# Preparing two neighbouring chunks of a DeltaNet scan as one pair, in tiles of eight heads

## The chip, the cores and the metric

One core of one Trainium2 chip runs the whole step. Its engines are called by short names throughout: PE is the matmul engine (TensorE), PEld its weight loads, DVE is VectorE, ACT is ScalarE, POOL is GpSimd, SP issues the DMAs. The metric is the device time of one execution in microseconds. Before the change the median of three runs is 2609.4 us (2607.69 to 2610.45).

## The reference

One layer of a hybrid backbone on 128 context tokens and 2048 latent tokens: a modulated RMSNorm, one input projection, then in parallel a bidirectional gated DeltaNet (4 heads of 128) and a gated MLP with spatial mixing, one output projection, then a squared-ReLU MLP of 1024 to 4096 and back. The change touches the DeltaNet alone:

```python
decay = jnp.where(incl, jnp.exp(jnp.where(incl, diff, 0.0)), 0.0)
a_mat = jnp.where(strict, jnp.einsum('bnhcd,bnhsd->bnhcs', k_beta, k) * decay, 0.0)
...
sol = lax.linalg.triangular_solve(a_mat + jnp.eye(DN_CHUNK, dtype=f32), rhs,
                                  left_side=True, lower=True, unit_diagonal=True)
...
qk = jnp.einsum('bnhcd,bnhsd->bnhcs', q, k) * decay
...
def step(S, xs):
    qd, kd, u_c, w_c, qk_c, gl = xs
    v_new = u_c - jnp.einsum('bhck,bhkv->bhcv', w_c, S)
    o = jnp.einsum('bhck,bhkv->bhcv', qd, S) + jnp.einsum('bhcs,bhsv->bhcv', qk_c, v_new)
    S = S * jnp.exp(gl)[..., None, None] + jnp.einsum('bhck,bhcv->bhkv', kd, v_new)
    return S, o
```

Per chunk and direction a triangular system is solved for each head (this needs nothing of the chunks before it), and then a short recurrence carries the state S from chunk to chunk. The kernel works with chunks of 128 tokens.

## The kernel before

The program has three stages: the input projection, the scan, the MLP. The trace has the scan's matmuls (those into the tile `pd`) from 462 to 1246 us. Only this stage is touched.

**Units.** There are 17 chunks and two directions d, so 34 units `unit(t, d)`. Each has a preparation (`prep`), which makes an explicit triangular inverse T for its four heads, and a recurrence (`scan`) of four steps. In the preparation, E holds the decays, KK the chunk's key products (with nbeta and the decay this becomes the negative triangular matrix, kept as the fp16 parts AH and AL), X and Y are the growing inverse and its transpose, P a scratch matrix, R a residual of one Newton step. The PE's groups in a preparation, with letters that this document uses for them, are

- **Y0**: four transposes of X into Y;
- five levels s = 2, 4, 8, 16, 32, each of a group **a** (four matmuls of AH with half of Y, 64 columns, L1065), a predicated copy by DVE into P (L1069), then groups **b** (P with X, L1076) and **c** (X with P, L1079), whose results ACT copies into Y (L1080) and X (L1081);
- the last level, 64, on quarters of the array: **m** (L1095) and **n** (L1103, L1105), matmuls of 64x64;
- **R** (eight matmuls, L1113 and L1114, DVE adds the identity, L1116) and **T** (five matmuls, L1122 and L1123, four ACT activations, L1126).

In this order each group waits for what DVE or ACT made of the group ahead of it. The four recurrence steps are called KS (state times keys, L992), TV (T times values), NS (new state) and O (output, L1179 and L1180); their operands are fp32.

**Fills.** Between these groups stand matmuls that nobody waits for at once: the gMLP's projections while the forward units run (L224 to L226 with `hH`, `hL`), the output projection while the backward units run (the same lines with `oH`, `oL`). A projection of one token tile is 24 matmuls of 512 columns, cut by `PARTS` into 9, 9 and 6; the output projection goes in pieces of 6.

**Order.** All steps are entered with a time in units (`at`, `spread`), sorted by it and recorded; `WINDOWS` holds the times. A unit's 18 preparation steps are spread from 2.46 to 0.03 units ahead of its recurrence, so that two or three units' preparations are interleaved. A scheduler then orders each engine's instructions by a timeline of its own; `emit` adds that a fill may not pass the last group of the preparation or recurrence that was entered ahead of it. DVE, ACT and POOL run their instructions strictly in the order that results.

**Buffers.** AH, AL, X and Y have three each (`BA`, `BX`), QK three, E, Es and KK share four. The five P tiles are shared by all units. They hold an identity, in which a level overwrites the same blocks each time; a unit that is the first of its direction (`fresh`) copies it anew.

Of the kernel before, what the change touches and what calls it, by code (L numbers as in the profile page):

```python
# [8 lines left out]
F32 = mybir.dt.float32  # L9
# [22 lines left out]
def interleave(*lists):  # L32
# [5 lines left out]
    for _, _, _, s in sorted(order, key=lambda e: e[:3]):  # L38
# [4 lines left out]
BA = 3  # L43
BX = 3
BT = 1
NS = 4
NE = 4
# [3 lines left out]
LATE = 0.5  # L51
PARTS = ((0, 3), (3, 6), (6, 8))
PL = 0
# [8 lines left out]
WINDOWS = [2.46, 0.03, -0.51, 1.06, -2.1, 18.16, 17.58, 18.3,  # L62
           2.63, -0.06, -0.18, 1.0, 1.36, 1.64, 1.66, 2.66, 3.17, 3.71]
# [3 lines left out]
def hybrid_step(  # L67
# [863 lines left out]
    with ExitStack() as ph:  # L931
# [17 lines left out]
        def f16(tag, bufs=1):  # L949
            return pp.tile([P, 4, P], F16, tag=tag, name=tag, bufs=bufs)  # L950
# [3 lines left out]

        def s32(name):
            return pp.tile([P, 4, P], F32, tag="e", name=name, bufs=NE)

# [6 lines left out]
        identq = f16("identq")  # L964
        V.tensor_copy(identq, bc4(ident16))
        pms = {s: f16(f"P{s}") for s in (2, 4, 8, 16, 32)}
# [15 lines left out]
        def unit(t, d, fresh=False, last=False):  # L982
# [11 lines left out]
            def prep_loads():  # L994
                u["gb"] = load_rows(g_d, t, d, "gr", 1, pp)
                u["KK"] = s32("KK")
                load(out=u["KK"], in_=kk_d[t])
                u["QK"] = q32("QK", 3)
                load(out=u["QK"], in_=qk_d[t])

            def scan_loads():
                for nm, src in (("kT", kT_d), ("qT", qT_d)):
                    u[nm] = q32(nm, 2)
                    load(out=u[nm], in_=src[:, :, t * P : (t + 1) * P])
                for nm, src in (("kt", kt_d), ("vt", vt_d)):
                    u[nm] = q32(nm, 2)
                    load(out=u[nm], in_=src[t * P : (t + 1) * P, :].rearrange("p (h d) -> p h d", h=H))
                u["eg"] = load_rows(eg_d, t, d, "eg", 3)
# [4 lines left out]
            @prep.append  # L1013
            def _():
                e = s32("E")
# [3 lines left out]
                es = s32("Es")  # L1019
                G.affine_select(out=es, in_=e, pattern=[[0, 4], [-sg, P]], compare_op=ALU.is_gt, fill=0.0,  # L1020
                                base=0, channel_multiplier=sg)
                G.affine_select(out=e, in_=e, pattern=[[0, 4], [sg, P]], compare_op=ALU.is_ge, fill=0.0,
                                base=0, channel_multiplier=-sg)
                u["Es"], u["E"] = es, e

            @prep.append
            def _():
                a = u["KK"]
                for h in range(H):
                    V.scalar_tensor_tensor(out=a[:, h, :], in0=a[:, h, :], scalar=col(nbeta, h),  # L1030
                                           in1=u["Es"][:, h, :], op0=ALU.mult, op1=ALU.mult)
# [3 lines left out]
            @prep.append  # L1035
            def _():
                u["AH"], u["AL"], u["X"] = f16("AH", BA), f16("AL", BA), f16("X", BX)
                A.copy(u["AH"], u["KK"])
                V.tensor_tensor(out=u["X"], in0=u["AH"], in1=bc4(sg2), op=ALU.mult)

            @prep.append
            def _():
                p = pd()
                for h in range(H):
                    T.matmul(p[:, h, :], u["X"][:, h, :], ident16, start=True, stop=True)
                u["Y"] = f16("Y", BX)
                A.copy(u["Y"], p)
                V.tensor_tensor(out=u["AL"], in0=u["KK"], in1=u["AH"], op=ALU.subtract)

            def level(s):  # L1050

                def half(ap, i):
                    return ap.rearrange("p h (a t b) -> p h a t b", t=2, b=s)[:, :, :, i, :]

                def packed(p, i):
                    return p[:, :, i * 64 : i * 64 + 64].rearrange("p h (a b) -> p h a b", b=s)

                yi = 1 - d

                @prep.append  # L1060
                def _():
                    p = pd()
                    pp, y = packed(p, 0), half(u["Y"], yi)
                    for h in range(H):
                        T.matmul(pp[:, h], u["AH"][:, h, :], y[:, h], start=True, stop=True)  # L1065
                    u["P"] = pms[s]
                    if fresh:
                        V.tensor_copy(pms[s], identq)
                    V.copy_predicated(out=half(u["P"], yi), mask=half(bc4(om[s]).bitcast(U16), yi), data=pp)  # L1069

                @prep.append
                def _():
                    p = pd()
                    py, px = packed(p, 0), packed(p, 1)
                    y, x, pm = half(u["Y"], yi), half(u["X"], 1 - yi), half(u["P"], yi)
                    pe = first_pe(lambda: [T.matmul(py[:, h], u["X"][:, h, :], pm[:, h], start=True, stop=True)  # L1076
                                           for h in range(H)])
                    for h in range(H):
                        T.matmul(px[:, h], u["P"][:, h, :], x[:, h], start=True, stop=True)  # L1079
                    A.copy(y, py)  # L1080
                    A.copy(x, px)  # L1081
                    if s == 8:
                        behind(lambda: V.tensor_tensor(out=u["QK"], in0=u["QK"], in1=u["E"], op=ALU.mult), pe)

            for s in (2, 4, 8, 16, 32):
                level(s)

            lo, hi = slice(0, 64), slice(64, P)
            ra, rb = (lo, hi) if d == 0 else (hi, lo)

            @prep.append
            def _():
                p = pd()
                for h in range(H):
                    T.matmul(p[ra, h, 0:64], u["AH"][rb, h, ra], u["Y"][rb, h, rb], start=True, stop=True)  # L1095
                u["P"] = f16("Pm", 1)
                A.copy(u["P"][ra, :, 0:64], p[ra, :, 0:64])

            @prep.append
            def _():  # L1100
                py, px = pd(), pd()
                for h in range(H):
                    T.matmul(py[ra, h, 0:64], u["X"][ra, h, ra], u["P"][ra, h, 0:64], start=True, stop=True)  # L1103
                for h in range(H):
                    T.matmul(px[rb, h, 0:64], u["P"][ra, h, 0:64], u["X"][ra, h, ra], start=True, stop=True)  # L1105
                A.copy(u["Y"][ra, :, rb], py[ra, :, 0:64])
                V.tensor_copy(u["X"][rb, :, ra], px[rb, :, 0:64])

            @prep.append
            def _():  # L1110
                p = pd()
                for h in range(H):
                    T.matmul(p[:, h, :], u["AH"][:, h, :], u["Y"][:, h, :], start=True, stop=False)  # L1113
                    T.matmul(p[:, h, :], u["AL"][:, h, :], u["Y"][:, h, :], start=False, stop=True)  # L1114
                u["R"] = f16("R", 1)
                V.tensor_tensor(out=u["R"], in0=p, in1=bc4(ident16), op=ALU.add)  # L1116

            @prep.append
            def _():
                p = pd()  # L1120
                for h in range(H):
                    T.matmul(p[:, h, :], u["X"][:, h, :], u["R"][:, h, :], start=h == 0, stop=False)  # L1122
                T.matmul(p, ident16, u["Y"], start=False, stop=True)  # L1123
                u["T"] = q32("T", BT)
                for h in range(H):
                    A.activation(u["T"][:, h, :], p[:, h, :], AF.Copy, scale=col(hbeta, h))  # L1126
# [15 lines left out]
            def _():  # L1142
                p = pd()
                pe = first_pe(lambda: quad(p, u["T"], u["vt"]))
                u["vn"] = q32("vn", BT)
# [51 lines left out]

        units = [unit(0, 0, True), unit(0, 1, True)] + [unit(t, 0, t == 1, t == NT - 1) for t in range(1, NT)]
        units += [unit(t, 1, t == NT - 1, t == 1) for t in range(NT - 1, 0, -1)]


# [216 lines left out]
        for i, u in enumerate(units):  # L1418
            w = p2 if i <= NT else p3
            at(i - 3 if i > PL else -12.5, u["prep_loads"])  # L1420
            at(i - 1, u["scan_loads"])
            n = len(u["prep"])
            for j, st in enumerate(u["prep"]):
                at(i - w[0] + (j + 0.5) * (w[0] - w[1]) / n, st, "prep")
# [36 lines left out]
        for j in range(len(wlist)):  # L1461
            at(-2 + 0.12 * j if j < KT else 16.4 + 0.12 * (j - KT), lambda j=j: split_next(j))
# [9 lines left out]
        spread(NT + 0.8, NT + 1.1, first, "fill")  # L1472
        spread(NT + 1.1, NT + 1.8, second, "fill")
        tend = max(e[0] for e in events if e[3] == "prep")
# [549 lines left out]
```

## Time and profile before

| what | value |
|---|---|
| median of the runs | 2609.4 us |
| the profiled execution | 2610.3 us, its span 2608.3 us |
| PE, PEld, DVE, ACT, POOL busy | 98%, 82%, 68%, 48%, 10% of the span |
| scan | 462 to 1246 us |

A row of a group gives the source line, engine, operation, output and inputs with shapes, the count, busy time, the mean of one in ns, and the idle time of the engine just before, with what ended it. In a timeline, the first column is the start in us and the second how long a row's instructions took together. A matmul's shown duration includes its way through the array, so a stream of them overlaps: their price is the distance from start to start. "PE busy" therefore also holds some waiting, and a group's idle time is a little less than what the wait cost.

### The profile page before, as it was taken

The page shows a single profiled execution, that of the slowest core. Times are in us where ns is not written, and L with a number is a line of the kernel's source. Part 1 is how long each engine was busy: PE and PEld are TensorE (multiplying, and loading weights), DVE is VectorE, ACT ScalarE, POOL GpSimd, SP SyncE. Part 2 cuts the span into 40 slices and gives each one's busy share as a digit, 9 for nine tenths or more (in the row PEclk, how much of TensorE's full clock was granted, in tenths as well). Part 3 has the DMA queues.
Part 4 walks back from the last instruction along what each step waited for, and adds up shares of the span by engine and source line. Part 5 has one row for each costly group of instructions (what it writes and reads, how often), then busy time and mean ns, then how long its engine had stood idle before and what let it go on. Part 6 is the DMA issues. An engine that isn't in the chain of part 4 may idle for free.

```text
span 2608.3 us, 44097 instructions
## 1 busy us (share of the span) xinstructions
PE 2563.6 (98%) x15330; PEld 2148.5 (82%) x15330; DVE 1771.7 (68%) x3587; ACT 1245.5 (48%) x3086; POOL 257.9 (10%) x478
## 2 busy tenths in 40 slices
PE   8999999999999999999999999999999999999998
PEld 4899999787888778778888888888887888888887
DVE  5767746666567878876588787677675545774875
ACT  4755555555555667764255553333342433242441
POOL 3112112111111122211000000000000000000000
PEclk9999999999999999999999999999999999999999
DMA  8966638655555667995778788545379978786773
GB/s 296 290 215 213 201 115 237 227 152 165 154 153 173 215 195 254 278 281 176 289 222 240 237 260 313 155 125 162 106 208 387 339 258 294 251 255 211 228 250 113
DMA packets 533860, 579.78 MB, mean 222 GB/s; under 512 B 35500, under 2 KB 366684, under 8 KB 530054
## 3 DMA queue, kind: packets, MB, share of 16 engines
q1 hardware_dynamic: 533638, 576.98, 69.2%
q8 instruction: 120, 1.97, 0.3%
q14 instruction: 102, 0.84, 0.1%
HBM read 397.62 MB, written 179.22 MB: 221 GB/s over the span
## 4 chain that ended last, share of the span: by engine, by line
PE 54%; DMA 5%; DVE 3%; ACT 2%; issue 1%; SPq 0%; DVEq 0%; POOLq 0%; POOL 0%; ACTq 0%
PE f L224 15%; PE f L225 15%; PE f L226 15%; PE pj L224 2%; PE pj L226 2%; PE pj L225 2%; DMA r<-in_w_ff_dram 1%; PE pd L992 1%; DMA x_d<-x 1%; DMA x<-x_d 1%; DMA traw<-in_w_ff_dram 1%; DMA zraw<-z_d 1%; PE pd L1179 0%; PE pd L1180 0%; DMA hop_d<-opL 0%
## 5 line engine op out<-in xcount | busy, mean ns | idle before, releaser
L224 PE MATMUL f<-hop,zH 128*128 128x512 f32 x960 | 373.6, 390 | 1.5 <-ACT zH L1527 1.4
L226 PE MATMUL f<-hop,zL 128*128 128x512 f32 x960 | 373.6, 390 | 0.0
L225 PE MATMUL f<-hop,zH 128*128 128x512 f32 x960 | 373.3, 389 | 0.1
L224 PE MATMUL f<-hop,wH 128*128 128x512 f32 x896 | 351.7, 393 | 1.0 <-ACT wH L1674 1.0
L225 PE MATMUL f<-hop,wH 128*128 128x512 f32 x896 | 349.0, 390 | 0.0
L226 PE MATMUL f<-hop,wL 128*128 128x512 f32 x896 | 344.0, 390 | 0.0
L1527 ACT CAST zH<-zraw 128x512 fp32r<-128x512 f32 x240 | 146.8, 620 | 284.6 <-DVE zraw L1521 83.9
L224 PEld LDWEIGHTS f<-hop,zH 128*128 128x128 f32 x960 | 180.2, 188 | 40.0 <-ACT zH L1527 2.8
L226 PEld LDWEIGHTS f<-hop,zL 128*128 128x128 f32 x960 | 180.2, 188 | 38.9 <-DVE zL L1521 1.7
L1521 DVE TENSOR_TENSOR zL<-zraw,zH 128x512 fp32r<-128x512 f32 x240 | 162.7, 688 | 71.6 <-ACT zH L1527 58.0
L225 PEld LDWEIGHTS f<-hop,zH 128*128 128x128 f32 x960 | 180.2, 188 | 37.6 <-DVE hop L1521 0.5
L224 PEld LDWEIGHTS f<-hop,wH 128*128 128x128 f32 x896 | 168.5, 188 | 35.8 <-ACT wH L1674 1.8
L226 PEld LDWEIGHTS f<-hop,wL 128*128 128x128 f32 x896 | 168.2, 188 | 35.6
L225 PEld LDWEIGHTS f<-hop,wH 128*128 128x128 f32 x896 | 168.6, 188 | 32.1
L226 PE MATMUL pj<-kH,wL 128*128 128x386 f32 (+2 forms) x568 | 190.6, 336 | 0.0
L224 PE MATMUL pj<-kH,wH 128*128 128x386 f32 (+2 forms) x568 | 189.2, 336 | 0.8 <-DVE cv L541 0.5
L225 PE MATMUL pj<-kL,wH 128*128 128x386 f32 (+2 forms) x568 | 189.4, 333 | 0.0
L182 POOL TENSOR_TENSOR r<-rsq,nhalf 128x1 f32<-128x1 f32 (+1 forms) x38 | 24.0, 631 | 1383.6 <-DVE rsq L181 1383.6
L1674 ACT CAST wH<-s 128x512 fp32r<-128x512 f32 x96 | 58.9, 620 | 171.4 <-DVE s L1521 158.1
L1069 DVE CAST_PREDICATED P<-om,pd 128x256 f16<-128x256 uint16 x170 | 72.2, 429 | 89.2 <-PE pd L1065 89.0
L541 DVE SCALAR_TENSOR_TENSOR cv<-pj,vec,cv 128x384 f32<-128x384 f32 (+2 forms) x164 | 87.2, 540 | 58.0 <-ACT cv L538 56.8
L224 PEld LDWEIGHTS pj<-kH,wH 128*128 128x128 f32 x568 | 107.1, 189 | 5.4 <-issue 5.0
(410 smaller groups left out, 5882.9 us busy)
## 6 DMA issues: line engine op xcount, KB each, us to landing
zraw<-z_d SPq DMA_DIRECT2D x212, 256.0 KB, 4.6
raw<-in_w_ff_dram SPq DMA_DIRECT2D x128, 256.0 KB, 4.6
hop<-hop_d SPq DMA_DIRECT2D x28, 1024.0 KB, 11.7
z_d<-c SPq DMA_DIRECT2D x96, 256.0 KB, 2.4
zraw<-s_d SPq DMA_DIRECT2D x96, 256.0 KB, 4.9
raw<-in_w_mod_dram SPq DMA_DIRECT2D x80, 256.0 KB, 4.6
r<-in_w_ff_dram SPq DMA_DIRECT2D x80, 256.0 KB, 5.5
s_d<-s SPq DMA_DIRECT2D x64, 256.0 KB, 3.0
```

The costliest lines, as they stand in the source:

```text
L182: G.tensor_tensor(out=out, in0=t[:np_, :n], in1=nhalf[:np_, :n], op=ALU.pow)
L224: T.matmul(ps, lh, rh, start=first and i == 0, stop=False, skip_group_check=more)
L225: T.matmul(ps, lh, rl, start=False, stop=False, skip_group_check=more)
L226: T.matmul(ps, ll, rh, start=False, stop=last and i == n - 1, skip_group_check=more)
L541: V.scalar_tensor_tensor(out=cv[:, o : o + m], in0=ps[:, s + sh : s + sh + m], scalar=convw[:, w, j : j + 1], in1=cv[:, o : o + m], op0=AL ...
L992: T.matmul(p[:, h, :], lhs[:, h, :], rhs[:, h, :], start=True, stop=True)
L1069: V.copy_predicated(out=half(u["P"], yi), mask=half(bc4(om[s]).bitcast(U16), yi), data=pp)
L1521: V.tensor_tensor(out=out, in0=a, in1=b, op=op)
L1527: A.copy(h, src)
L1674: A.copy(h, s2)
```

## The change

- `pair(us)` takes two neighbouring units and prepares them as one: AH, AL, X, Y, P and R are tiles of eight heads, one buffer each, so one pair is prepared at a time. The groups a, b, c, m, n have eight matmuls each instead of four, and one DVE or ACT instruction evicts all eight heads. Only R, T and Y0 are evicted by chunk; of Y0 the second chunk's half is copied by DVE instead of ACT.
- A pair's preparation has 16 steps over two units, at steps of an eighth of a unit (15 PE steps per unit before, so 30 for two units). The recurrence's four steps stand on the same grid.
- `PARTS` cuts the gMLP's fills into four pieces of 6 matmuls.
- The P tiles are reset by `clear` when a half changes its direction.
- E isn't masked any more: POOL masks KK, and QK after it was multiplied by E. That product moves from behind the level s = 8 to a step that precedes the pair's levels.
- QK has four buffers, eg two (three before), KK two of its own, E one.

The diff, cut:

```diff
-PARTS = ((0, 3), (3, 6), (6, 8))
+PARTS = ((0, 2), (2, 4), (4, 6), (6, 8))
...
-WINDOWS = [2.46, 0.03, -0.51, 1.06, -2.1, 18.16, 17.58, 18.3,
-           2.63, -0.06, -0.18, 1.0, 1.36, 1.64, 1.66, 2.66, 3.17, 3.71]
+WINDOWS = [2.0, 0.0, -0.285, 0.715, -2.1, 18.9, 17.58, 18.3,
+           2.0, 0.0, -0.285, 0.715, 1.36, 1.64, 1.6875, 2.6875, 3.17, 3.71]
...
+        def pd8():
+            return psd.tile([P, 8, 64], F32, tag="d", name="pd", bufs=4)
...
+        def clear(lo, hi):
+            for pm in pms.values():
+                V.tensor_copy(pm[:, lo:hi], ident16.unsqueeze(1).to_broadcast([P, hi - lo, P]))
...
+        def pair(us):
+            g = {}
+            ds = [u["d"] for u in us]
+            spans = [(0, 8, ds[0])] if ds[0] == ds[1] else [(0, 4, ds[0]), (4, 8, ds[1])]
+            stale = [c for c in range(2) if left[c] != ds[c]]
...
+            def heads():
+                for c in stale:
+                    clear(4 * c, 4 * c + 4)
+                for nm in ("AH", "AL", "X"):
+                    g[nm] = f16(nm)
+                for c, u in enumerate(us):
+                    A.copy(mine("AH", c), u["KK"])
+                    V.tensor_tensor(out=mine("X", c), in0=mine("AH", c), in1=bc4(sg2), op=ALU.mult)
...
+                    (V.tensor_copy if c else A.copy)(mine("Y", c), p)
...
+                    p = packed(pd8(), w)
+                    for lo, hi, d in spans:
+                        y = half(g["Y"], 1 - d, w)
+                        for h in range(lo, hi):
+                            T.matmul(p[:, h], g["AH"][:, h, :], y[:, h], start=True, stop=True)
+                    for lo, hi, d in spans:
+                        mask = om[w].unsqueeze(1).to_broadcast([P, hi - lo, P]).bitcast(U16)
+                        V.copy_predicated(out=half(pms[w][:, lo:hi], 1 - d, w), mask=half(mask, 1 - d, w),
+                                          data=p[:, lo:hi])
...
+            c = i % 2
+            at(i - c - 3.3 + 0.5 * c if i > 1 else -12.5 + c, u["prep_loads"])
             for j, st in enumerate(u["prep"]):
-                at(i - w[0] + (j + 0.5) * (w[0] - w[1]) / n, st, "prep")
+                at(i - c - 2.9 + 0.45 * c + 0.13 * j, st, "prep")
+            if c == 0:
+                heads, steps = pairs2[i // 2]
+                at(i - 2.0, heads, "prep")
+                n = len(steps)
+                for j, st in enumerate(steps):
+                    at(i - w[0] + (j + 0.5) * (w[0] - w[1]) / n, st, "prep")
```

How this moves instructions is read from the two built programs.

On PE, in the forward part of the scan, where a preparation reaches the 64x64 level (L1103, the groups n). Before:

```order
L1079 LDWEIGHTS P_5735
L1079 MATMUL pd<-X,P_5735 128x64
L1103 LDWEIGHTS X
L1103 MATMUL pd<-Pm,X 64x64
L1103 LDWEIGHTS X
L1103 MATMUL pd<-Pm,X 64x64
```

After the change (L219 to L221 are the fill's lines, L1210 those of n, and R is the name of the buffer that Pm now shares):

```order
L219 MATMUL pm<-wH,hH 128x512
L220 MATMUL pm<-wL,hH 128x512
L221 MATMUL pm<-wH,hL 128x512
L1210 LDWEIGHTS X
L1210 MATMUL pd<-R,X 64x64
L1210 LDWEIGHTS X
L1210 MATMUL pd<-R,X 64x64
```

The group n stood right behind a group c of another unit, and stands now behind a fill, with twice as many matmuls in it.

On PE, in the forward part, at the first level (P_5734 before and P_5732 after are the P tile of s = 2). Before, from the last matmul of a group a to the b that reads that tile:

```order
L1065 MATMUL pd<-Y,AH 128x64
L224 MATMUL pm<-wH,hH 128x512
L225 MATMUL pm<-wL,hH 128x512
L226 MATMUL pm<-wH,hL 128x512
L224 MATMUL pm<-wH,hH 128x512
L225 MATMUL pm<-wL,hH 128x512
L226 MATMUL pm<-wH,hL 128x512
L224 MATMUL pm<-wH,hH 128x512
L225 MATMUL pm<-wL,hH 128x512
L226 MATMUL pm<-wH,hL 128x512
L1076 LDWEIGHTS X
L1076 MATMUL pd<-P_5734,X 128x64
```

After, the second half of the pair's first a (L1159) and its b (L1173):

```order
L220 MATMUL pm<-wL,hH 128x512
L221 MATMUL pm<-wH,hL 128x512
L1159 LDWEIGHTS AH
L1159 MATMUL pd<-Y,AH 128x64
L1159 LDWEIGHTS AH
L1159 MATMUL pd<-Y,AH 128x64
L1159 LDWEIGHTS AH
L1159 MATMUL pd<-Y,AH 128x64
L1159 LDWEIGHTS AH
L1159 MATMUL pd<-Y,AH 128x64
L1173 LDWEIGHTS X
L1173 MATMUL pd<-P_5732,X 128x64
```

The pair's first a is split: four matmuls, a fill, the other four. The fill stands ahead of the second half, and none is left between it and b.

On DVE, in the forward part, between two predicated copies. Before, from the copy of one level to the next copy in the queue:

```order
L1069 COPY_PREDICATED P_5738<-om_190,pd 128x8x32
L1271 SCALAR_TENSOR_TENSOR ug<-pm,vec,ug 128x128 x4
L1157 TENSOR_TENSOR qT<-qT,eg 128x512
L1245 SCALAR_TENSOR_TENSOR gw<-gw,pj 128x512
L1069 COPY_PREDICATED P_5735<-om_187,pd 128x64x4
```

After, from Y0's second half to the copies of s = 2 and s = 4:

```order
L1139 CAST Y<-pd 128x512
L1294 SCALAR_TENSOR_TENSOR gw<-gw,pj 128x512
L1162 COPY_PREDICATED P_5732<-om_186,pd 128x256x2
L1149 TENSOR_TENSOR AL<-KK,AH 128x512 x2
L1066 TENSOR_TENSOR qT<-qT,eg 128x512
L1077 TENSOR_TENSOR S<-pd,se 128x512
L1162 COPY_PREDICATED P_5733<-om_187,pd 128x128x4
```

The copies are half as many and twice as wide, and other work of the scan still stands in the queue ahead of them.

More of the change, by code (lines that the diff above doesn't have):

```diff
@@ L50 @@
 NF = 5
-LATE = 0.5
-PARTS = ((0, 3), (3, 6), (6, 8))
-PL = 0
+LATE = 0.1
+PARTS = ((0, 2), (2, 4), (4, 6), (6, 8))
 HT = 4
@@ L947, in pj, with f16 @@
             return pm1() if len(nj) % 4 in (1, 2) else psj.tile([P, 512], F32, tag="j", name="pj", bufs=2)
-        def f16(tag, bufs=1):
-            return pp.tile([P, 4, P], F16, tag=tag, name=tag, bufs=bufs)
+        def pd8():
+            return psd.tile([P, 8, 64], F32, tag="d", name="pd", bufs=4)
+        def f16(tag):
+            return pp.tile([P, 8, P], F16, tag=tag, name=tag, bufs=1)
         def q32(tag, bufs=1, pool=None):
             return (pool or dl).tile([P, 4, P], F32, tag=tag, name=tag, bufs=bufs)
-        def s32(name):
-            return pp.tile([P, 4, P], F32, tag="e", name=name, bufs=NE)
         def load_rows(src, t, d, tag, bufs, pool=None):
@@ L962, in load_rows @@
             return gb
-        identq = f16("identq")
-        V.tensor_copy(identq, bc4(ident16))
-        pms = {s: f16(f"P{s}") for s in (2, 4, 8, 16, 32)}
+        pms = {w: f16(f"P{w}") for w in (2, 4, 8, 16, 32)}
+        def clear(lo, hi):
+            for pm in pms.values():
+                V.tensor_copy(pm[:, lo:hi], ident16.unsqueeze(1).to_broadcast([P, hi - lo, P]))
+        clear(0, 8)
         def behind(fn, name):
@@ L980, in first_pe, with unit @@
             return [x.name for x in tc.nc.cur_bb.bb.instructions[start:] if x.engine == mybir.EngineType.PE][0]
-        def unit(t, d, fresh=False, last=False):
+        def unit(t, d, last=False):
             u = {}
@@ L1030, in _ @@
                     V.scalar_tensor_tensor(out=a[:, h, :], in0=a[:, h, :], scalar=col(nbeta, h),
-                                           in1=u["Es"][:, h, :], op0=ALU.mult, op1=ALU.mult)
+                                           in1=u["E"][:, h, :], op0=ALU.mult, op1=ALU.mult)
+                G.affine_select(out=a, in_=a, pattern=[[0, 4], [-sg, P]], compare_op=ALU.is_gt, fill=0.0,
+                                base=0, channel_multiplier=sg)
                 G.affine_select(out=a, in_=a, pattern=[[0, 4], [1, P]], compare_op=ALU.not_equal, fill=-1.0,
@@ L1036, in _ @@
             def _():
[L1037 to L1126, printed above, removed]
+                q = u["QK"]
@@ L1128, in _ @@
+                V.tensor_tensor(out=q, in0=q, in1=u["E"], op=ALU.mult)
+                G.affine_select(out=q, in_=q, pattern=[[0, 4], [sg, P]], compare_op=ALU.is_ge, fill=0.0,
+                                base=0, channel_multiplier=-sg)
             @scan.append
@@ L1202, in f2_steps @@
+        pairs2 = [pair(units[i : i + 2]) for i in range(0, len(units), 2)]
         def f2_steps(t):
@@ L1471, in hybrid_step @@
         first, second = o_steps(units[1])
-        spread(NT + 0.8, NT + 1.1, first, "fill")
-        spread(NT + 1.1, NT + 1.8, second, "fill")
-        tend = max(e[0] for e in events if e[3] == "prep")
+        spread(NT + 0.9, NT + 1.3, first, "fill")
+        spread(NT + 1.4, NT + 2.65, second, "fill")
+        tend = len(units) - 1.01
         at(tend + 0.01, swap_right)
```

122 lines of the change are left out of this document (102 added, 20 removed).

## The prediction

> **What bounds the kernel now.** I read the windows by stage first, then the list of waits on the scan's own tile `pd`, then PE's timeline.
>
> ```profile
> span 2608.3 us, 44097 instructions
> ```
> ```profile
> core 0: us, PE busy (x) PEld busy (x) DVE busy (x) ACT busy (x) POOL busy (x), PEclk, DMA share, GB/s
> 462.00:1246.00 784.00, 760.23 (x6488) 625.58 (x6487) 551.01 (x1413) 473.40 (x1344) 143.41 (x170) 1.00 0.65 203
> ```
>
> The window of the scan says that PE works 760 of 784 us; DVE is busy 551 (70%), ACT 473. So PE sets the time, and the change can only win what PE loses: waits, and time that its matmuls take beyond their stream. The matmuls themselves stay: in both built programs the scan has 2040 of 64 columns, 408 of 64x64 and the same fp32 ones. The stages outside the scan keep their PE order, so they stay at their times. The waits, from the tile's view (us, times):
>
> ```profile
> its engine sat idle before it (us, times) until:
>   DVE P L1069: 14.2, 18
>   ACT Y L1080: 4.6, 9
>   DVE X L1039: 1.6, 1
>   DVE rr L1338: 1.2, 1
>   ACT Y L1106: 0.9, 4
> ```
>
> That is 22.5 us in 33 waits, 14.2 of them for the predicated copy P. A wait costs more than the idle time shown, and after a long one PE is slow for a while. Both are in the timeline:
>
> ```profile
> 485.95 0.29 PE L1065 MATMUL pd<-Y,AH 128*128 128x64 f16 x4
> ...
> 486.20 0.28 PE L1079 MATMUL pd<-X,P 128*128 128x64 f16 x4
> 486.28 0.42 DVE L1069 CAST_PREDICATED P<-om,pd 128x256 f16<-128x256 uint16 x1 [0.71 <-PE pd L1065]
> ...
> 486.75 0.28 PE L1076 MATMUL pd<-P,X 128*128 128x64 f16 x4 [0.28 <-DVE P L1069]
> ...
> 1131.02 0.37 PE L1076 MATMUL pd<-P,X 128*128 128x64 f16 x4 [3.24 <-DVE P L1069]
> ...
> 1132.42 0.63 PE L226 MATMUL pm<-wH,oL 128*128 128x512 f32 x1
> 1132.84 0.63 PE L224 MATMUL pm<-wH,oH 128*128 128x512 f32 x1
> ...
> 1137.35 0.40 PE L224 MATMUL pm<-wH,oH 128*128 128x512 f32 x1
> ```
>
> Group c at 486.20 takes 0.12 without a wait; b comes 0.55 later, so 0.43 is lost where 0.28 is shown as idle: 0.15 more per wait. All waits then cost 22.5 + 33 x 0.15 = 27.5 us, those for P 14.2 + 18 x 0.15 = 17, the others 10.5. After the idle time of 3.24 us the fills stand 0.42 apart until about 1137; a fill is otherwise 0.23 (rows below). Nine fills at 0.2 and eight fp32 matmuls of half that are 2.6 us more. Waits cost this scan about 30 us in all.
>
> **The change, part by part. Switching.** PE's stream has a price at each change of kind:
>
> ```profile
> 599.27 0.40 PE L226 MATMUL pm<-wH,hL 128*128 128x512 f32 x1
> 599.60 0.31 PE L1095 MATMUL pd<-Y,AH 64*64 64x64 f16 x4
> 599.84 0.29 PE L1076 MATMUL pd<-P,X 128*128 128x64 f16 x4
> ...
> 604.21 0.48 PE L224 MATMUL pm<-wH,hH 128*128 128x512 f32 x1
> 604.53 0.40 PE L225 MATMUL pm<-wL,hH 128*128 128x512 f32 x1
> 604.76 0.40 PE L226 MATMUL pm<-wH,hL 128*128 128x512 f32 x1
> 605.82 0.28 PE L1079 MATMUL pd<-X,P 128*128 128x64 f16 x4
> 605.94 0.47 PE L1179 MATMUL pd<-S,qT 128*128 128x128 f32 x2
> 606.24 0.39 PE L1180 MATMUL pd<-vn,QK 128*128 128x128 f32 x2
> 606.46 0.39 PE L1179 MATMUL pd<-S,qT 128*128 128x128 f32 x2
> ...
> 607.58 0.39 PE L1180 MATMUL pd<-vn,QK 128*128 128x128 f32 x2
> 607.72 0.48 PE L224 MATMUL pj<-wH,hH 128*128 128x512 f32 x1
> 608.04 0.39 PE L225 MATMUL pj<-wL,hH 128*128 128x512 f32 x1
> ```
>
> From start to start: a fill within a stream 0.23 (604.53 to 604.76). The fill ahead of a 64x64 group takes 0.33, so entering costs 0.10; four 64x64 matmuls ahead of another kind take 0.24 where four of 64 columns take 0.12 (605.82 to 605.94), so leaving costs about 0.11. The first fill behind fp16 takes 0.32, 0.09 more; the first fp32 product 0.30 instead of 0.22, 0.08 more. From fp32 into a fill costs nothing: 0.14 instead of 0.22, then 0.32 instead of 0.23. I counted the changes of kind in the two orders. 64x64 groups are entered 68 times before and 35 after: 33 x 0.21 = 6.9 us. Fills behind fp16: 183 and 146, 37 x 0.09 = 3.3. fp32 products behind fp16: 147 and 129, 18 x 0.08 = 1.4. fp32 into a fill: 73 and 134, at nothing. Sum 11.6; I take 11. The counts only fall, so a loss is excluded; if leaving 64x64 is dearer with its longer groups, half remains, so 6 to 12.
>
> **Waits for P.** The chain from 486.04 (last start of that a) is 0.24 to DVE, 0.42 for the copy, 0.05 to b: 0.71. The copy of eight heads isn't in the trace: at least 0.42 (no dearer), at most 0.84 (as two). The nearest rows:
>
> ```profile
> L1069 DVE CAST_PREDICATED P<-om,pd 128x256 f16<-128x256 uint16 x170 | 72.2, 429 | 89.2 <-PE pd L1065 89.0
> L1116 DVE TENSOR_TENSOR R<-pd,ident 128x512 f16<-128x512 f32 x34 | 23.2, 682 | 4.1 <-PE pd L1114 4.1
> L1068 DVE COPY P<-identq 128x512 f16<-128x512 f16 x15 | 4.2, 288 | 5.4 <-PE pd L1079 5.4
> ```
>
> R reads as many fp32 elements from `pd` and writes as many fp16, so I take 0.68: a to b becomes 0.97. What covers it is the PE work between. Before, by the order and the prices above, the median cover was 2.6 us, since fills were nine long and other units' groups stood there. After, 42 of the 80 groups behind the first pair have one fill of six: 5 x 0.23 + 0.32 = 1.47. Margin 0.5. Another 25 have more. In 12 the second half of a stands directly ahead of its b (the second order of the change), so each waits 0.97 less its own 0.03: 11 us, certain in kind, 8 to 13 by the bounds of the copy.
>
> How late DVE comes to a copy decides the rest.
>
> ```profile
> DVE P L1069 <- PE pd L1065: 89.0, 64, 3.8
> ```
>
> This row of waits says that DVE stood ready for 64 of the 170 copies; for 106 it still had other work. After, a copy that comes over 0.5 late stalls PE at 42 places. At the third order four operations of about 0.68 stand between the copies of s = 2 and s = 4: 2.7 us, against b and c 0.5, NS 1.0, a fill 1.47 and a 0.24 of PE, 3.2: it just fits, and with four products more in the queue, as in other pairs, it doesn't. Adding DVE's work between all copies, each at its group's mean, against PE's: ordinary pairs lose about 4 us; where the direction turns, 27 us of DVE work are queued for 22 us of PE (ten resets of 0.29 among them), which with its neighbours loses 11. With the 11 above that is 26 us. The same sum for the kernel before gives 21 where the trace shows 17, so 26 may be high; lateness as it is now, met by the thinner cover, would give 33. I take 25, from 14 to 35.
>
> **The other waits, 10.5 now.** Y behind b and c now always has a fill and c itself ahead of its reader: 1.7 us for a chain that the R row bounds at 0.24 + 0.68 + 0.05. The recurrence's groups have two fills and more between. The first pair starts with a fill at each step, where several of the present waits lie. I take 4, bounds 1 and 10. Half speed after a long wait is likely at the turn of direction: 1 of 2.6.
>
> **Edits that I cost at nothing, with their cover.** Fewer ACT and DVE instructions free engines that are not the bound; without this cover they would be worth what P and Y waits hold already. POOL keeps three masks per unit, on a queue that is busy 143 of 784 us; KK's two now stand in line ahead of AH, some six us early by the written times. DVE takes half of Y0, 0.68 per pair. Single AH, X and Y mean that the next pair's X waits for T: two DVE products, 0.9 us, under one fill of 1.47 and T's end; margin 0.5, and gone when DVE is late. QK's load for the unit four ahead waits for O on SP's queue, with the loads of kT and vt behind it, and its product with E now stands ahead of KS's evictions on DVE.
>
> ```profile
> DMA to landing us min/median/max: 3.5/3.7/4.5
> ```
>
> A QK load lands 3.7 us after its issue; PE issues two fills, R and T, about 4.5 us, from O to KS. Level, and KS has two fills to spare.
>
> Sum: -11 for switching; waits 25 + 4 + 1 = 30 against 30 before, so 0. 2610.3 - 11 = 2599.3, and the median of the runs lies 0.9 under the profiled execution: 2599 rounded up.
>
> **Rivals.** (1) *The waits go.* If DVE takes the copies at once, only the 11 us of zero cover and 4 us others remain: 15 instead of 30, and 2609.4 - 11 - 15 = 2583. For it: the regular order, a fill at every other step. Against it: the 106 of 170 copies.
>
> (2) *Nothing to measure.* DVE is as late as now: 33 for P, 6 others, 2 for the clock, 41 against 30: 2609.4 - 11 + 11 = 2609. The thinner cover speaks for it, 1.5 against 2.6 us; against it, half as many groups wait.
>
> (3) *Slower.* The pair's start: X, Y0's half and the first copy all go through DVE, behind the gMLP's statistics, with one buffer each and no other pair to work on. If that chain comes 2 us later than assumed in each of 16 pairs, 32 us come on top, and waits of over 3 us halve PE's rate as at 1131: 2599 + 32 less what is counted = 2625. It decides when the first b of a pair waits over 2 us on the median; at 1 us the forecast holds. The 3.24 us at 1131 show that such waits happen. [...]
>
> **How the numbers follow.** 0.2% of 2609 us, 5.2 us, is about what a measurement tells from no change. The forecast (2590 to 2604) has 0.45, rival 1 0.20, rival 2 0.21, rival 3 0.14. So faster 0.65, same 0.21, slower 0.14. The range 2582 to 2613 holds the forecast, rival 2 and most of rival 1; waits of 14 to 45 us span it.
>
> **What would show it.** Right: 64x64 groups entered half as often; waits for P of about 0.9 us at the first level of twelve pairs; Y waits nearly gone; the scan 11 us shorter with about the same idle time. Wrong: P waits at later levels in most pairs, or one wait of over 3 us at the turn with PE at half rate behind it, or no wait at the first level.

## The result, and the profile after

The changed kernel takes 2624.8 us (median of 4 runs, 2620.1 to 2627.3); the kernel before, run beside it, 2609.9. The ratio is 1.0054, with a 95% interval from 1.0037 to 1.0072: slower by some 14 us, where 10 us less were forecast. The profiled execution of the changed kernel has a span of 2622.6 us, 14.3 more than before.

First the page's head, then the window of the scan (columns as in the prediction), which now ends some 12 us later:

```profile
span 2622.6 us, 43865 instructions
```
```profile
462.00:1262.00 800.00, 761.61 (x6511) 624.77 (x6511) 541.45 (x1341) 451.94 (x1145) 147.15 (x174) 0.99 0.65 202
```

The window is cut at 1262 instead of 1246, since the last O product starts at 1257 instead of 1245. Of the 16 us that it is longer, 1.4 are PE busy and the rest is idle time. To split the difference, I measured the scan in every trace from three matmuls ahead of the first Y0 product to the first matmul of the MLP, and priced each PE instruction at the tenth percentile of the start-to-start times of its kind between the same two neighbours, over all traces. That sum is the stream; the rest is waiting. All the "scan" times below are this stretch.

| | scan us | stream | waiting |
|---|---|---|---|
| before | 805.9 | 741.4 | 64.6 |
| after | 817.9 | 731.2 | 86.7 |

So the stream did become 10 us shorter, and the waiting 22 us longer: 12 us in the scan. The other 2 us are not the change's: the first fill starts at 407.9 us before and at 410.7 after, behind the same instructions, and at 405.6 to 409.9 in the traces of the experiments.

The waits, from the view of the scan's tile `pd` on PE, after (who ended the idle time, us, times):

```profile
  DVE P L1162: 18.0, 24
  ACT R L1201: 7.2, 4
  ACT wH L190: 5.4, 1
  DVE X L1130: 2.9, 5
  ACT Y L1182: 1.8, 5
  DVE R L1228: 1.1, 3
  ACT gw L1263: 0.5, 1
  ACT Y L1217: 0.4, 1
```

P's are about those of the forecast. New are the long ones: 7.2 us for the Pm copy, which is written in the buffer R, and one wait of 5.4 at the scan's start (the profile puts it down to the cast of wH, but Y0 reads X, which DVE finished only 0.05 us ahead of it, at 473.93). The three longest, 3.17, 2.98 and 5.42 us, have one origin, in the timeline around 946 and 1176, and at the start:

```profile
939.77 0.69 ACT L1016 ACTIVATE E<-gr,gcol 128x128 f32<-128x128 f32 x2
942.51 0.43 SPq L956 DMA_DIRECT2D gr<-g_d  x1
946.18 0.43 PE L1198 MATMUL pd<-Y,AH 64*64 64x64 f16 x8
948.96 1.28 ACT L1016 ACTIVATE E<-gr,gcol 128x128 f32<-128x128 f32 x4 [4.62 <-DMA gr<-g_d]
950.74 0.58 ACT L1201 CAST R<-pd 64x512 f16<-64x512 f32 x1
951.38 0.31 PE L1210 MATMUL pd<-R,X 64*64 64x64 f16 x5 [3.17 <-ACT R L1201]
...
1176.88 1.28 ACT L1016 ACTIVATE E<-gr,gcol 128x128 f32<-128x128 f32 x4 [2.37 <-DMA gr<-g_d]
1178.69 0.58 ACT L1201 CAST R<-pd 64x512 f16<-64x512 f32 x1
1179.32 0.42 PE L1210 MATMUL pd<-R,X 64*64 64x64 f16 x5 [2.98 <-ACT R L1201]
```
```profile
467.08 1.29 ACT L1016 ACTIVATE E<-gr,gcol 128x128 f32<-128x128 f32 x4 [1.24 <-DMA gr<-g_d]
...
472.85 0.62 ACT L1129 CAST AH<-KK 128x512 f16<-128x512 f32 x1 [3.48 <-POOL KK L1027]
...
473.98 0.61 PE L1138 MATMUL pd<-ident,X 128*128 128x128 f16 x4 [5.42 <-ACT wH L190]
```

The g row of a pair's second chunk can only be loaded when the first chunk's E has read it, since `gr` has one tile: at 942.51, behind the E of 939.77. It lands 6 us later. Until then ACT stands at the second E, 4.62 us, and behind that E in its queue is the copy R, whose 64x64 products were done at 946.6. At the start the same late row sets off E, KK, masks, AH and X, and PE waits 5.42 us for the second Y0. Behind the waits at 474 and 1179 PE runs at half rate for some us (granted clock 0.50 and 0.53, rows in the last section); these are called slow stretches below. The waits of ACT show the total (us, times, longest), first after, then the only such row of the kernel before:

```profile
ACT E L1016 <- DMA gr<-g_d: 13.5, 5, 5.0
```
```profile
ACT E L1017 <- DMA hL<-hL_d: 5.1, 1, 5.1
```

In both kernels the very first E stands some 5 us for a DMA (after, at 458.32), ahead of the scan's first product. New are the other four waits, 8.5 us.

On DVE the load of QK does the like on the return pass:

```profile
1045.00 0.69 DVE L1033 TENSOR_TENSOR QK<-QK,E 128x512 f32<-128x512 f32 x1 [1.49 <-DMA QK<-qk_d]
1045.61 0.68 DVE L1228 TENSOR_TENSOR R<-pd,ident 128x512 f16<-128x512 f32 x1
1046.34 0.38 PE L1237 MATMUL pd<-R,X 128*128 128x128 f16 x4 [0.47 <-DVE R L1228]
```
```profile
DVE QK L1033 <- DMA QK<-qk_d: 13.1, 11, 2.0
```

R is late because DVE stood at QK, and X, further down in the queue, is still late at 1051. Last, the first level of a pair, as forecast (the first row is the second half of a, the last is b, with no fill between):

```profile
734.76 0.29 PE L1159 MATMUL pd<-Y,AH 128*128 128x64 f16 x4
735.09 0.73 DVE L1162 CAST_PREDICATED P<-om,pd 128x512 f16<-128x512 uint16 x1 [0.42 <-PE pd L1159]
...
735.87 0.40 PE L1173 MATMUL pd<-P,X 128*128 128x64 f16 x8 [0.82 <-DVE P L1162]
```

### The profile page after: what moved, and what is told of

It is laid out like the page before. It is cut to its first block, busy times and chain, and to the rows that moved or that the text cites. A ratio compares the mean times of both kernels' runs of the same rounds, so it can differ in the third digit from the quotient of the medians.

```text
span 2622.6 us, 43865 instructions
## 1 busy us (share of the span) xinstructions
PE 2561.7 (98%) x15330; PEld 2143.1 (82%) x15330; DVE 1758.6 (67%) x3507; ACT 1220.3 (47%) x2877; POOL 258.5 (10%) x478
## 4 chain that ended last, share of the span: by engine, by line
PE 52%; DMA 3%; DVE 1%; issue 1%; ACT 1%; SPq 0%; DVEq 0%; POOLq 0%; ACTq 0%
PE f L219 16%; PE f L221 16%; PE f L220 16%; DMA t_d<-r 1%; PE pj L219 1%; PE pj L221 1%; PE pj L220 1%; DMA r<-in_w_ff_dram 1%; PE pd L991 0%; DMA traw<-in_w_ff_dram 0%; DMA x_d<-x 0%; PE pd L1088 0%; PE f L855 0%; PE pd L1089 0%; DMA zraw<-z_d 0%
## 5 line engine op out<-in xcount | busy, mean ns | idle before, releaser
L219 PE MATMUL f<-hop,zH 128*128 128x512 f32 x960 | 373.6, 390 | 2.0 <-ACT zH L1582 2.0
L221 PE MATMUL f<-hop,zL 128*128 128x512 f32 x960 | 373.9, 390 | 0.0
L219 PE MATMUL f<-hop,wH 128*128 128x512 f32 x896 | 351.6, 393 | 0.5 <-ACT wH L1729 0.5
L221 PE MATMUL f<-hop,wL 128*128 128x512 f32 x896 | 344.0, 390 | 0.0
L219 PEld LDWEIGHTS f<-hop,zH 128*128 128x128 f32 x960 | 180.2, 188 | 40.3 <-ACT zH L1582 3.3
L221 PEld LDWEIGHTS f<-hop,zL 128*128 128x128 f32 x960 | 180.2, 188 | 39.5 <-DVE zL L1576 2.2
L221 PEld LDWEIGHTS f<-hop,wL 128*128 128x128 f32 x896 | 168.2, 188 | 35.7
L219 PEld LDWEIGHTS f<-hop,wH 128*128 128x128 f32 x896 | 168.5, 188 | 35.0 <-ACT wH L1729 1.1
L221 PE MATMUL pj<-kH,wL 128*128 128x386 f32 (+2 forms) x568 | 190.6, 335 | 0.0
L219 PE MATMUL pj<-kH,wH 128*128 128x386 f32 (+2 forms) x568 | 189.2, 336 | 0.4 <-DVE kH L486 0.3
L1162 DVE CAST_PREDICATED P<-om,pd 128x512 f16<-128x512 uint16 (+1 forms) x90 | 60.2, 674 | 80.9 <-PE pd L1159 80.7
L219 PEld LDWEIGHTS pj<-kH,wH 128*128 128x128 f32 x568 | 107.1, 189 | 5.0 <-issue 4.5
```

The source lines that it names most:

```text
L219: T.matmul(ps, lh, rh, start=first and i == 0, stop=False, skip_group_check=more)
L221: T.matmul(ps, ll, rh, start=False, stop=last and i == n - 1, skip_group_check=more)
L1162: V.copy_predicated(out=half(pms[w][:, lo:hi], 1 - d, w), mask=half(mask, 1 - d, w), data=p[:, lo:hi])
```

## The experiments

Three causes are on the table: the single g row tile, the split first a, the load of QK. The rival to all is that DVE is simply short of time with copies twice as long. The diff also moves the times of other steps (`LATE`, the weight splits, the last output steps); no run takes these apart. The first three experiments take one cause away each, the fourth all three. Ratios are to the kernel before on the same chip, with 95% intervals.

**The g row in two tiles.** E is computed in place, so that two tiles fit.

```diff
-                u["gb"] = load_rows(g_d, t, d, "gr", 1, pp)
+                u["gb"] = load_rows(g_d, t, d, "gr", 2, pp)
...
-                u["E"] = e = q32("E", 1, pp)
+                u["E"] = e = u["gb"]
```

> The changed kernel with E computed in place in the tile of its g row, and two such tiles instead of one of each: the same bytes, the same work, PE's order the same but for one product. Theory A (the second chunk's g row waits for the single tile that the first chunk's E still reads, and ACT stands behind it): the waits of 5.4 us at 474, 3.2 at 951 and 3.0 at 1179 go, with the slow stretches behind the first and the last (2.8 and 2.6 us): 17 us at most, about 14 expected, so 2611 instead of 2625. Theory B (what is late is the chain behind the row: KK's product on DVE, two masks on POOL, AH on ACT, X on DVE, some 6 us): the waits stay within 1.5 us of their size, 2621 or more.

Ratio 1.0023 (1.0012 to 1.0034), scan 809.3: 8.6 us less. The wait at 951 is gone, and so is the slow stretch behind 1179, where 1.94 us of waiting are left (granted clock 1.00 from 1171.6 to 1175). At the start 2.43 us are left, now for X, and behind them a shorter slow stretch (granted clock 0.57 from 466.5 to 470.5; the fill at 467.19 takes 0.63 us, the one at 463.71 took 0.39). ACT waits for the row once, ahead of the scan; but QK's wait on DVE grew from 13.1 to 21.3 us, and with it the waits for R and X:

```profile
ACT gr L1016 <- DMA gr<-g_d: 5.7, 1, 5.7
```
```profile
DVE QK L1033 <- DMA QK<-qk_d: 21.3, 14, 3.8
```
```profile
  DVE X L1130: 6.0, 7
...
  DVE R L1228: 3.1, 3
```

Theory A holds in kind, and not in size. Of the 5.4 us that are missing from its 14, the pairs between 962 and 1143 gave back 3.7, behind the next late load; the others are what is left at 474 and 1179. The edit also gives E a second buffer; that the row, and not E's own buffer, came last is read from the DMA that ends the waits at 948.96 and 1176.88.

**Fills behind the whole of a step.** A fill depends on the first matmul of the last step; here, in steps of eight, on the eighth.

```diff
-                hist.append(pe[0])
+                hist.append(pe[7] if kind == "prep" and len(pe) == 8 else pe[0])
```

> The changed kernel with the fills held behind the last matmul of a step of eight, so that group a is never split and a fill stands between every a and its b. Theory A (12 first-level waits of 0.98 us are lack of cover alone): they go, and 15 fewer entries into a fill save about 1 us more: 12 us less, 2613. Theory B (DVE comes late to these copies, or Y's half on DVE comes late to the whole a): half of the waits come back ahead of a or b, 2618 or more.

Ratio 1.0023 (1.0014 to 1.0033), scan 805.9: 12.0 us less in the profiled execution, theory A's number; by the ratios it is some 8. P's waits go from 18.0 us in 24 to

```profile
  ACT wH L190: 8.7, 1
  DVE P L1162: 8.1, 8
```

with copies as long as before. The first row is the price: the two Y0 of the first pair now stand together, so the 12 fills between them no longer cover the late second one (8.7 instead of 5.4). About 10 of the 12.0 us lie in the pairs that had the split a. The slow stretch behind 1179 went too (granted clock 1.00 from 1173 to 1179), for which theory A has no reason, and a new one came behind a wait of 3.20 us for P at 931 (0.50 from 931.3 to 935); these two largely cancel.

**QK's product later.** It moves 0.3 of a chunk back for the second chunk, behind R and X on DVE.

```diff
-                at(i - c - 2.9 + 0.45 * c + 0.13 * j, st, "prep")
+                at(i - c - 2.9 + 0.45 * c + 0.13 * j + (0.3 if c and j == 2 else 0), st, "prep")
```

> The changed kernel with the product of QK and E of a pair's second chunk 0.3 of a chunk later in the order, nothing else. Theory A (on the return pass DVE stands 1.5 us ahead of that product, for QK's load, and R, the copies for P and X queue behind it): the waits of 0.5 us for R and 0.5 for X in the pairs between 1000 and 1150 go, some 1.2 to 2.2 us per pair in five pairs: 2617 to 2619. Theory B (DVE is short of time there for the output's norm and projection, whatever QK does): the same waits appear elsewhere, 2623 to 2626.

Ratio 1.0034 (1.0021 to 1.0046), scan 812.3: 5.7 us less. No row for R is left in the waits, and X falls from 2.9 to

```profile
  DVE X L1130: 2.1, 3
```

The sum matches theory A, but only 3.2 of the 5.7 us lie in the return pass that it speaks of; the others lie at the start (1.3) and around the turn (1.1 in the pair at 951), and no theory here names them. DVE does the same work on the return pass (207 us busy of 290 after, 210 of 290 here); only the order in its queue changed.

**All three.**

> The three edits together: g row in two tiles with E in place, fills behind the whole of a step of eight, QK's product 0.3 of a chunk later for the second chunk. If the three causes are separate, their gains add: 14 + 12 + 6 = 32 us, 2593, about 16 under the kernel before. If they share one slack (DVE's or ACT's queue), less than 22 us come back: 2603 or more.

Ratio 0.9944 (0.9931 to 0.9956), 2591.1 us; scan 789.9, which is 28.0 us less than after. The three alone gave 8.6 + 12.0 + 5.7 = 26.3: within a few us the gains add, and with QK moved the g row's gain is no longer given back. The stream is 731.3, as after; all 28 us are waits.

```profile
  DVE P L1162: 5.4, 8
  ACT R L1201: 3.5, 5
  DVE X L1130: 2.8, 2
...
```

Where the gains lie, pair by pair, is read from the time between a pair's first Y0 product and the next pair's (us against the changed kernel, negative is shorter; the first column begins and the last ends with the scan; 951 lies in pair 11, 1179 in pair 16):

| | pair 1 | 2 to 10 | 11 | 12 to 15 | 16 | 17 |
|---|---|---|---|---|---|---|
| g row in two tiles | -4.8 | -1.2 | -3.5 | +3.7 | -2.3 | -0.4 |
| fills behind whole steps | -0.6 | -5.0 | +2.2 | -3.1 | -4.5 | -1.1 |
| QK's product later | -1.3 | -0.1 | -1.1 | -2.8 | +0.4 | -0.8 |
| all three | -5.0 | -7.4 | -4.9 | -3.6 | -5.9 | -1.2 |

So pairs with half as many groups, single AH, X and Y and fills of six are faster than the kernel before, with DVE's copies as long as after; what made the change slower is in three lines beside them.

**E behind the Pm copy, in the changed kernel.** This takes the queue apart from the buffer: the g row keeps one tile, but on ACT the E that waits for it stands behind the copy.

```diff
-                at(i - c - 2.9 + 0.45 * c + 0.13 * j, st, "prep")
+                at(i - c - 2.9 + 0.5 * c + 0.13 * j, st, "prep")
```

> The changed kernel with the prep steps of a pair's second chunk 0.05 of a chunk later, nothing else: on ACT its E, which waits for the g row, then stands behind the copy of Pm (in buffer R) instead of ahead of it; the g row keeps its single tile. Theory A (the two waits at 951 and 1179 come from ACT standing at E with that copy behind it): both go, 3.2 and 3.1 us and the 2.6 us of slow stretch, while the 5.6 us at the scan's start stay: 7 to 9 us less, 1.002 of the kernel before. Theory B (the late g row delays the whole pair): the waits turn up at the next Y0, for X, and the time stays at 1.005.

Ratio 1.0016 (1.0006 to 1.0026), scan 810.8: 7.1 us less, of which 4.7 in the pair at 951 and 2.3 in the pair at 1179, where theory A has them. The wait at 951 is gone, but the other became 2.42:

```profile
944.52 0.58 ACT L1201 CAST R<-pd 64x512 f16<-64x512 f32 x1
...
945.74 0.34 PE L1210 MATMUL pd<-R,X 64*64 64x64 f16 x5
...
1170.12 0.62 ACT L873 CAST opH<-d 128x512 fp32r<-128x512 f32 x1 [2.55 <-DMA hop_d<-opH]
1170.76 0.58 ACT L1201 CAST R<-pd 64x512 f16<-64x512 f32 x1
...
1171.39 0.31 PE L1210 MATMUL pd<-R,X 64*64 64x64 f16 x5 [2.42 <-ACT R L1201]
```

At 1170 another instruction at the head of ACT's queue waits for a store, and the copy again stands behind it; theory A had this wait gone, and the gain there is a shorter wait and a shorter slow stretch (granted clock 0.69 from 1171.4 to 1176). What costs is not the g row as such but a copy that PE needs behind an instruction that waits for a DMA. In the profiles before and after, ACT's and DVE's instructions all start in the order of the built program (2795 and 3587 of them before, 2586 and 3507 after); behind the rows at 948.96 and 1170.12 the copy starts at 950.74 and 1170.76.

**Thin fills in the kernel before.** PARTS alone becomes (0, 2), (2, 4), (4, 6), (6, 8).

> The kernel before with its fills in four parts of six matmuls instead of 9, 9 and 6, the only edit. The prediction's rival of nothing to measure held that cover of 1.5 us instead of 2.6 would raise the waits for P of the kernel before from 17 to 33 us: then 12 to 18 us slower, 1.005 to 1.007. If cover hardly matters because DVE mostly stands ready, the waits stay at 15 to 20 us and only more entries into fills cost, 3 us: 1.001.

Ratio 0.9990 (0.9980 to 1.0001), scan 802.7. The waits for P do not rise (14.2 us in 18 before):

```profile
  DVE P L1069: 12.5, 13
```

Thin cover as such costs nothing in the kernel before, with its copies of four heads. This kernel also tests the prices of switching: it has 227 fills behind fp16 instead of 183 and 137 fp32 products behind fp16 instead of 147, by the prediction's prices 44 x 0.09 - 10 x 0.08 = 3.2 us; its stream is 745.8, 4.5 more than before.

**Thick fills in the changed kernel.** PARTS alone becomes (0, 3), (3, 6), (6, 8).

> The changed kernel with its fills in three parts of 9, 9 and 6 matmuls as before, the only edit. Fewer pieces than steps: in the order some 15 more groups a stand directly ahead of their b, with no fill between. If a missing fill costs 0.97 us wherever it is missing, the waits for P rise by 15 us, less 4 for fewer entries into fills: 1.009 to 1.011 of the kernel before. If thicker fills elsewhere absorb DVE's lateness, it ends level with the changed kernel, 1.005.

Ratio 1.0113 (1.0098 to 1.0129), 2634.6 us. The time is the first theory's, the cause only partly: the profiled execution is a short one (span 2625.0), its scan 5.7 us longer than after, and of the 15 more waits for P there are five; R's product waits too (1.1 us in 3 after).

```profile
  DVE P L1162: 22.7, 29
  DVE R L1228: 5.1, 8
```

Pair by pair, pairs 2 to 10 are 14.4 us longer, which is about the first theory's size, while the pairs at 951 and 1179 are 6.5 shorter. That missing fills cost is shown. The other three executions are 6 to 11 us longer than the profiled one, at a granted clock of 0.994 to 0.995 over the run instead of 0.997: 0.002 to 0.003 of 2630 us is 5 to 8 us, so more time at half rate may be most of it. That is an estimate; only the short execution has a trace.

**Fills begun earlier, on top of all three.** `p2[4]`, the fifth number of `WINDOWS` and the time of the first fill, goes from -2.1 to -2.5.

> The three edits together (g row in two tiles, whole steps of eight, QK's product later) and the fills begun 0.4 of a chunk earlier, so that 24 more of them run ahead of the first Y0 product. Theory A (what is left at the scan's start, 2.4 and 2.1 us of waits for the first two X, is only lack of cover for a chain of E, KK, masks, AH and X that starts when the g row lands): both waits go and the fills, thinned by 24 of some 1000, cost nothing elsewhere: 4 us less than with the three edits, 0.993 of the kernel before. Theory B (the fills missing later are the cover of other steps): the gain is given back in the middle of the scan, 0.994 to 0.996.

Ratio 0.9957 (0.9944 to 0.9971), no better than 0.9944. The waits for the first X are gone (4.5 us in the three edits together), but

```profile
479.13 0.60 ACT L1293 ACTIVATE gw<-pm 128x512 f32<-128x512 f32 x1 [6.03 <-DMA gate_d<-gw]
479.62 0.64 ACT L1182 CAST Y<-pd 128x256 f16<-128x256 f32 x2
...
480.04 0.65 PE L1159 MATMUL pd<-Y,AH 128*128 128x64 f16 x8 [5.07 <-ACT Y L1182]
```

with the gates closer together, ACT stands at one for the store of the tile it reuses, and Y behind it. Neither theory had this; it is the mechanism of 951 with another transfer.

**Whole steps everywhere**, on top of all three: `hist.append(pe[-1])`.

> The three edits together, but with the fills held behind the last matmul of every step, not only of steps of eight: b and c of the first pair, the products R and the first steps of the return pass stay whole too. If split steps cost by their switches and by b without cover, 2 to 4 us less than with the three edits, 0.993. If the waits there are for data that come late anyway, PE waits longer where a fill would have run: 0 to 3 us more, 0.995.

Ratio 0.9931 (0.9919 to 0.9943), scan 782.5, 7 us less than with the three, all of it in the first pair; the intervals of the two ratios overlap.

**And E behind the Pm copy**, on top of that (0.5 for 0.45 as above).

> The kernel with the three edits and whole steps everywhere, and E of the second chunk behind the copy of Pm on ACT. Four waits of 0.7 us for that copy on the return pass are left in the kernel without this last edit: they go, 2.5 us less, 0.992 of the kernel before. If ACT's work is only pushed on to the next reader (Y of the next step, AH of the next pair), it stays at 0.993.

Ratio 0.9922 (0.9909 to 0.9936), scan 783.3: PE's waits for the copy R fall from 2.2 us to 0.5, those for X and Y rise from 2.3 to 4.0; within what the runs can tell, nothing.

**And the fills begun 0.15 of a chunk earlier** (p2[4] = -2.25).

> The kernel with the three edits, whole steps everywhere and E behind the copy of Pm, with the fills begun 0.15 of a chunk earlier (12 more ahead of the first Y0). With 0.4 of a chunk ACT stood 6 us at a gate's tanh for the store of the tile it reuses, with the copy for Y behind it. Theory A (12 fills, 2.7 us, cover most of the 3.8 us of waits for the first X, and the gate's tile is free by then): 3 us less than without, 0.991 of the kernel before. Theory B (the gate's tile is as late as with 24): 0.992 to 0.994.

2583.7 us, ratio 0.9910 (0.9897 to 0.9924): the fastest here, though its interval overlaps that of the kernel without this last edit; 23 us under the kernel before beside it and some 38 under the changed kernel by the ratios. The longest waits left on `pd`, of 8.6 us in all:

```profile
  DVE P L1162: 3.4, 6
  DVE X L1130: 1.6, 3
  ACT R L1201: 1.5, 1
...
```

## Why the prediction was wrong

The sum said -11 for switching and 30 us of waits before and after. By its own terms (idle time, 0.15 per wait, the clock):

| term | forecast | measured |
|---|---|---|
| switching | -11 (6 to 12) | -10 |
| waits for P | 25 (14 to 35) | 18.0 + 24 x 0.15 = 21.6 |
| other waits | 4 (1 to 10) | 19.3 + 20 x 0.15 = 22.3 |
| half clock | 1 | 5.4 |
| waits, sum | 30 | 49.3 |

- **Switching: right.** 64x64 groups are entered 35 times instead of 68, the stream is 10 us shorter, and the prices held in a second kernel (thin fills), if a little low.
- **Waits for P at the first level: right**, in twelve pairs: 1.00 to 1.18 us from the last a to b in eleven, and 2.27 in the one at the turn of direction (916); with fills behind whole steps about 10 us came back in these pairs.
- **DVE's lateness: over-estimated.** The copy takes 0.70 us, close to the 0.68 assumed (mean of the 80 of eight heads), but 14 us of waits beyond the first level were forecast and some 8 came. The kernel with thin fills suggests why the rival of nothing to measure was too dark: with copies of four heads, P's waits do not grow when the cover shrinks.
- **The other waits: the step that failed.** "I take 4, bounds 1 and 10": 22. Y's waits did go, as argued, to 2.2 us in 6. What came was in no term: 7.2 for the Pm copy, 5.4 for the second Y0, 4.0 for X and R. The changed prep times were on show, 0.45 of a chunk between the E of the two chunks of a pair, through a `gr` with one tile; the prediction followed POOL's masks, AH, X and Y, but not the g row.
- **QK costed at nothing: wrong by 3 to 6 us.** The reader whose wait was checked was PE's O and KS ("KS has two fills to spare"); the one that paid was what stands behind QK's product on DVE, R and X. QK's product later gave 5.7 us, 3.2 of them on the return pass.
- **The clock: right in kind, too small.** Two stretches behind waits (granted clock 0.50 and 0.53) instead of 0.4 of one, 2.7 us each where 2.6 was read off the trace of before.
- Measured terms give -10 + 49.3 - 30 = 9 us of the scan's 12; 1.2 more are waits of fills for the projection's tmp, and about 2 lie in delays under 0.06 us each.
- **Rival 3** named the right side, 2625, for a reason that fell; that its number is the measured one is luck. Its condition, a first b that waits over 2 us on the median, was not met (1.01 from start to start), and AH, X and Y keep their single buffers in the kernels that beat the one before. The single buffer that mattered was `gr`. That waits of over 3 us halve PE's rate rested on the one at 1131 (3.24 us); behind the 3.17 us at 951 the granted clock was 1.00.
- **What would show it:** 64x64 entries, first-level waits and Y as said; the scan 12 us longer instead of 11 shorter. Of the signs named for being wrong, the long wait near the turn came (951), though with PE at full rate behind it.

## What to carry to other kernels

Where two pieces of work are moved next to each other, list every tile with one buffer that both pass through, inputs first, and for each late load name the instruction that waits for it and then what stands behind that instruction in its queue: that copy, not the load, is what PE pays for. Cover is a matter of order before it is one of size: a fill that may slip into the middle of a step leaves the step's end bare, and one line that ties the fill to the step's last matmul gave about 10 us in the pairs concerned. A merge can be right and its surroundings wrong: the stream's 10 us were there all along, under 22 us of new waits.

## What the runs showed of the hardware

The length of an idle gap does not decide alone whether PE falls to half rate. After the gap of 3.17 us at 951 the granted clock stays full; after 2.98 at 1179 and 5.42 at 474 it is half (the eighth column):

```profile
951.40:957.00 5.60, 5.60 (x58) 4.98 (x58) 3.65 (x10) 3.39 (x12) 1.28 (x2) 1.00 0.98 351
1179.40:1186.00 6.60, 6.60 (x39) 5.88 (x39) 3.63 (x8) 2.46 (x8) 1.27 (x2) 0.53 0.99 313
474.00:482.00 8.00, 7.46 (x40) 5.49 (x41) 4.44 (x8) 1.17 (x3) 0.00 (x0) 0.50 0.90 287
```

In the fastest kernel the rate falls behind a gap of 1.52 us, 1.7 us after its end (0.63 us for two fp32 products, where two at 952.19 in the changed kernel take 0.39; the granted clock is 0.50 from 1144.7 to 1148):

```profile
1142.94 0.31 PE L1210 MATMUL pd<-R,X 64*64 64x64 f16 x5 [1.52 <-ACT R L1201]
...
1144.65 0.63 PE L1089 MATMUL pd<-vn,QK 128*128 128x128 f32 x2
```

The clock records have half rate for 10.24 us from 472.25 and for 6.83 us from 1178.81 in the changed kernel's scan, and for 6.83 us from 1130.33 in the scan before. These lengths, and the 706.56 us between the two starts in the changed kernel, are whole multiples of a third of the first, 3.413 us (3, 2, 2 and 207 times). How long a gap must be, the traces do not show: half rate came behind 1.52 us in one and not behind 3.17 in another; what else counts is open.
